# Output projection of a two-layer trunk: the last two token tiles add x in one DVE step, and half of their affine steps for h go to ACT

## The chip, the cores and the metric

The kernel runs on one core of a Trainium2 chip. TensorE (PE, with its weight loads as PEld), VectorE (DVE), ScalarE (ACT) and GpSimd (POOL) each work off a queue of their own in order; all DMAs of this kernel are issued from SyncE's queue (SP), in order as well. The metric is the device time of one execution in microseconds (us), as the median of several. The profile comes from one execution.

## The reference, cut to what matters

Two layers work on 128 context tokens (`x_prompt`) and 1024 latent tokens (`x_sample`), 1024 channels each. What follows is one layer, cut to the parts around the change:

```python
mod = (silu(cvec) @ w_mod + b_mod).reshape(-1, 1, 3 * D_MODEL)
shift, scale, gate = jnp.split(mod, 3, axis=-1)
h = rms_norm(x, g_pre) * (1.0 + scale) + shift
fx, fz, rq, rk, rv, rz, aq, ak, av, az, mg = split_columns(h @ w_in)
...
merged = ga * (ya @ w_pa) + gb * (yb @ w_pb) + gc * (yc @ w_pc)
out = merged @ w_out
x = x + gate * rms_norm(out, g_post)
```

`rms_norm(v, g)` is `v * (mean(v*v) + 1e-6) ** -0.5 * g`, the mean over the 1024 channels. So after the output projection of layer 0 each token gets a new x, and from it the h of layer 1, on which every projection of layer 1 rests.

## The kernel before

**Tiles.** The 1152 tokens are nine tiles of 128 (t = 0 is the context, t = 1 to 8 the latents). h is held in SBUF for all tokens, transposed (channels on partitions), as a pair of rounded high and low parts, HH and HL. A projection is three matmuls for each of eight channel groups (high by high, low by high, high by low): `proj_n` (L223) gives 128 tokens by 512 columns, 24 matmuls, `proj_t` (L214) gives 128 columns by 384 tokens. Weights come as units of 128x1024: a DMA into one of two `raw` tiles, a cast on ACT (L174), a subtraction on POOL (L175).

**The output projection** (L1195 to L1247) runs over the nine tiles. For one tile: `proj_n` twice, columns 0 to 511 into a bank `pj` (of two; for tiles 0 to 3 other banks serve too) and 512 to 1023 into a bank `sl` (of two). ACT squares each half and sums it (L1219). DVE adds the two sums (L1222) and scales them, POOL raises the mean to the power -1/2 (`rstd_of`, L244 to L249), which gives r. DVE then makes acc * r * gate for each half (L1239: reads PSUM and the gate row `gpb`), POOL adds x to that over 1024 columns (L1242), and SP stores x: to `x_d` (scr_x) in layer 0 (L1246), to the output in layer 1 (L1244). One case is written otherwise: the last tile of the last layer (`end`, L1223). There DVE multiplies each half by the gate as soon as its projection is there (`xg`, L1226 and L1229), and when r has come one DVE step for each half makes xg * r + x (L1232), with a store for each half.

**h for layer 1.** In layer 0 `make_h` (L259 to L278) follows for each tile: ACT squares and sums x (L254), DVE and POOL make the power, DVE scales x by it (L256), PE transposes eight 128x128 blocks (L268) into two banks `tr`, DVE makes the affine step with scale `smn` and shift `shn` for each block (L272, four for each half), ACT casts the half to HH (L277), DVE subtracts to get HL (L278).

**What comes next.** Layer 1 begins with `nat_group` (L510): again `proj_n` for t = 0 to 8, into the same two `pj` banks. ACT empties the bank of t = 0 (L525); for t > 0 DVE empties it with the rotary step (`rope`, L482 and L488), which reads the table `ropet`, and ACT takes the rest (L539). After that come units for the Fourier branch by `proj_t` (L641, evacuated by L643 and L644). Between them run steps of the modulation for the next layer, `mod_steps` (L422): loads `mw` (L411), products on DVE (L435, L437), a reduction (L453), stores to `scr_mod` (L463), and small constants of the retention branch (L561 to L612).

**Order and memory.** The order on each engine is worked out when the program is built: a planner with its own model of time puts an instruction into its engine's queue when that model has it ready, the one traced first being preferred. On the chip each queue then runs in that order and waits at its head. SBUF pools are stacked from the left and from the right end, and a tile in a pool that is opened later waits for the release of every earlier tile whose bytes it covers. In the program's memory map (bytes of a partition) the left side in layer 0's output projection is `wo1` (129152 to 137344), `wo2` (to 170112) and `wo3` (170112 to 197184; last in it are the small tiles of `make_h` and `hf`, whose order is that of their first use). On the right side layer 1 opens `wx` (212960 to 229344) and `mix` (197600 to 212960). The table `ropet` is the first tile of `mix`: 197600 to 201696. It is loaded once for layer 1, by L508 (512 KB). A tile `xg` takes 4096 bytes; before, only layer 1's `wo3` holds one.

Of the kernel before, what the change touches and what calls it, by code (L numbers as in the profile page):

```python
# [11 lines left out]
AF = mybir.ActivationFunctionType  # L12
# [4 lines left out]
P = 128  # L17
D = 1024
KT = 8
NT = 9  # L20
# [62 lines left out]
def hybrid_step(ctx, tc, ins, cst, outs):  # L83
    nc = tc.nc
    PE, ACT, DVE, POOL, SP = nc.tensor, nc.scalar, nc.vector, nc.gpsimd, nc.sync
# [7 lines left out]
    def pool(name, bufs=1, side=None, space=None):  # L93
        kw = dict(name=nm(name), bufs=bufs, reuse_waits="tile")
        if side is not None:
            kw["side"] = side
        if space is not None:
            kw["space"] = space
        return tc.tile_pool(**kw)

    def dram(name, shape):
        return nc.dram_tensor(name, shape, F32, kind="Internal").ap()

    def mk(pl, shape, tag, dt=F32, **kw):
        return pl.tile(shape, dt, tag=tag, name=nm(tag), **kw)
# [6 lines left out]
    x_d = dram("scr_x", (TOK, D))  # L112
# [26 lines left out]
    def tr(shape):  # L139
        return bank("tr", 2, shape)  # L140
# [8 lines left out]
    sh = mk(const, [P, KT, 2], "sh")  # L149
    sm = mk(const, [P, KT, 2], "sm")  # L150
    siluc = mk(const, [P, KT, 2], "siluc")
    shn = mk(const, [P, KT, 2], "shn")
    smn = mk(const, [P, KT, 2], "smn")
# [5 lines left out]
    def f(ap):  # L159
        return ap.bitcast(F32)  # L160
# [62 lines left out]
    def proj_n(units, t, acc):  # L223
        tok = slice(t * P, (t + 1) * P)
        for k in range(KT):
            hi, lo = units[k // 2]
            a, b = HH[:, k, tok], HL[:, k, tok]
            PE.matmul(acc, a, hi[:, k % 2, :], start=(k == 0), stop=False)  # L228
            PE.matmul(acc, a, lo[:, k % 2, :], start=False, stop=False)  # L229
            i = PE.matmul(acc, b, hi[:, k % 2, :], start=False, stop=(k == KT - 1))  # L230
        anchor["pe"] = i.ins
# [12 lines left out]
    def rstd_of(pl, ss, n, inv_n, eps, tag):  # L244
        v = mk(pl, [P, n], tag + "v", bufs=2)
        DVE.tensor_scalar(v, ss, inv_n, eps, op0=ALU.mult, op1=ALU.add)
        r = mk(pl, [P, n], tag + "r", bufs=2)
        POOL.tensor_tensor(out=r, in0=v, in1=mhalf[:, :n], op=ALU.pow)
        return r  # L249

    def norm_x(pl, xt):
        xh = mk(pl, [P, D], "xh", bufs=2)
        ss = mk(pl, [P, 1], "ss", bufs=2)
        ACT.activation(xh, xt, AF.Square, accum_out=ss)  # L254
        r = rstd_of(pl, ss, 1, 1.0 / D, EPS, "hr")
        DVE.tensor_scalar(xh, xt, r, None, op0=ALU.mult)  # L256
        return xh

    def make_h(pl, xt, t, sm, sh):  # L259

        s = 0 if t == 0 else 1
        xh = norm_x(pl, xt)
        tok = slice(t * P, (t + 1) * P)
        for half in range(2):
            pt = tr([P, 4, P])
            for kk in range(4):
                k = half * 4 + kk
                PE.transpose(pt[:, kk, :], xh[:, k * P : (k + 1) * P], ident)  # L268
            hf = mk(pl, [P, 4, P], "hf")
            for kk in range(4):  # L270
                k = half * 4 + kk
                DVE.tensor_scalar(  # L272
                    hf[:, kk, :], pt[:, kk, :], sm[:, k, s : s + 1], sh[:, k, s : s + 1],
                    op0=ALU.mult, op1=ALU.add,
                )
            ks = slice(half * 4, half * 4 + 4)
            ACT.copy(HH[:, ks, tok], hf)  # L277
            DVE.tensor_tensor(out=HL[:, ks, tok], in0=hf, in1=f(HH[:, ks, tok]), op=ALU.subtract)  # L278
# [216 lines left out]
    for l in range(DEPTH):  # L495
        last = l == DEPTH - 1
# [704 lines left out]
        wo3 = est.enter_context(pool("wo3"))  # L1201
# [3 lines left out]
        for t in range(NT):  # L1205
            s = 0 if t == 0 else 1
            xo = mk(wo3, [P, D], "xo", bufs=2)
            if l == 0:
                SP.dma_start(xo, ins["x_prompt"][0] if t == 0 else ins["x_sample"][0, (t - 1) * P : t * P, :])
            else:  # L1210
                SP.dma_start(xo, x_d[t * P : (t + 1) * P, :])
            tokP = slice(t * P, (t + 1) * P)
            accs = []
            ss = mk(wo3, [P, 2], "oss2", bufs=2)
            xn = mk(wo3, [P, D], "xh", bufs=2)
            for n, W in enumerate((W0, W1)):
                acc = (sl if n else (pj, pj, sc, pv)[t] if t < 4 else pj)([P, 512])
                proj_n(W, t, acc)
                ACT.activation(xn[:, n * 512 : n * 512 + 512], acc, AF.Square, accum_out=ss[:, n : n + 1])  # L1219
                accs.append(acc)  # L1220
            s1 = mk(wo3, [P, 1], "s1", bufs=2)
            DVE.tensor_tensor(out=s1, in0=ss[:, 0:1], in1=ss[:, 1:2], op=ALU.add)  # L1222
            end = last and t == NT - 1  # L1223
            if end:
                xg = mk(wo3, [P, D], "xg")
                DVE.tensor_tensor(out=xg[:, 0:512], in0=accs[0], in1=gpb[:, s, 0:512], op=ALU.mult)  # L1226
            r = rstd_of(wo3, s1, 1, 1.0 / D, 4.0 * EPS, "xr")
            if end:
                DVE.tensor_tensor(out=xg[:, 512:D], in0=accs[1], in1=gpb[:, s, 512:D], op=ALU.mult)  # L1229
                for n in range(2):  # L1230
                    ns = slice(n * 512, n * 512 + 512)
                    DVE.scalar_tensor_tensor(  # L1232
                        out=xo[:, ns], in0=xg[:, ns], scalar=r, in1=xo[:, ns], op0=ALU.mult, op1=ALU.add
                    )
                    SP.dma_start(y_s[0, (t - 1) * P : t * P, ns], xo[:, ns])
                continue
            for n in range(2):
                ns = slice(n * 512, n * 512 + 512)
                DVE.scalar_tensor_tensor(  # L1239
                    out=xn[:, ns], in0=accs[n], scalar=r, in1=gpb[:, s, ns], op0=ALU.mult, op1=ALU.mult  # L1240
                )
            POOL.tensor_tensor(out=xo, in0=xo, in1=xn, op=ALU.add)  # L1242
            if last:
                SP.dma_start(y_p[0] if t == 0 else y_s[0, (t - 1) * P : t * P, :], xo)  # L1244
            else:
                SP.dma_start(x_d[t * P : (t + 1) * P, :], xo)  # L1246
                make_h(wo3, xo, t, smn, shn)  # L1247
# [31 lines left out]
```

## Time and profile before

| | us |
|---|---|
| median of 3 runs | 2003.23 |
| lowest and highest of them | 2001.77 and 2006.81 |
| the profiled execution, whole | 2004.05 |
| its span, first to last instruction | 2002.3 |
| of the span: PE busy | 1961.0 |
| DVE busy | 991.0 |
| ACT busy | 678.1 |
| POOL busy | 549.0 |

Between the span and the profiled execution's time lie 1.75 us that the profile doesn't show. The busy times are sums over all stages. The stage that the diff touches in layer 0 lies at about 929 to 1063 us of the span (output projection and the h of layer 1, with layer 1's first projection beginning at 1030); that in layer 1 is the last of the span. In a view in order of time a row has start, duration, engine, line, operation, out and in; a bracket at its end gives how long the engine stood idle before it and what ended that. The views of waits give who waited for whom, the sum in us, how often, and the longest.

### The profile page before, as it was taken

The numbers are of one execution on the slowest core, as the hardware profiler recorded it, in microseconds if no ns is written. First come the engines' busy times: TensorE is split into PE (matmuls) and PEld (weight loads), VectorE is DVE, ScalarE is ACT, GpSimd is POOL, SyncE is SP. The second block draws the span as 40 slices with busy tenths as digits, with TensorE's granted clock in tenths as the row PEclk, the third lists the DMA queues.
The fourth block names the chain that finished last, engine by engine and source line by source line (L and its number), as shares of the span: only waits on it lengthen the run. The fifth ranks groups of instructions, "written<-read, shape, count | busy, mean of one in ns | idle before, by whom it ended". The sixth has DMA issues, their size and how long they took to land.

```text
span 2002.3 us, 29865 instructions
## 1 busy us (share of the span) xinstructions
PE 1961.0 (98%) x11046; PEld 1794.2 (90%) x11046; DVE 991.0 (49%) x2557; ACT 678.1 (34%) x1536; POOL 549.0 (27%) x424
## 2 busy tenths in 40 slices
PE   8999999999999999999999999999999999999998
PEld 2898878999999999999878878899999999999987
DVE  4626556556667765104675272444556665410411
ACT  3522111234555444114331212022455555421411
POOL 2222232111112332444441214122111222333342
PEclk9999999999999999999999999999999999999999
DMA  9323554353334334323344145234422433422142
GB/s 298 105 72 98 149 139 135 102 178 105 97 116 123 117 103 137 91 89 128 116 135 101 58 103 162 74 115 129 125 82 88 121 100 97 143 92 83 60 153 85
DMA packets 245186, 230.53 MB, mean 115 GB/s; under 512 B 37920, under 2 KB 215856, under 8 KB 244784
## 3 DMA queue, kind: packets, MB, share of 16 engines
q1 hardware_dynamic: 245040, 228.62, 37.6%
q8 instruction: 87, 1.43, 0.3%
q14 instruction: 59, 0.48, 0.1%
HBM read 170.14 MB, written 58.42 MB: 114 GB/s over the span
## 4 chain that ended last, share of the span: by engine, by line
PE 88%; DMA 4%; DVE 3%; ACT 1%; issue 1%; SPq 1%; POOL 1%; DVEq 0%; POOLq 0%; ACTq 0%
PE pj L218 13%; PE pj L220 13%; PE pj L219 13%; PE pj L228 5%; PE pj L229 5%; PE pj L230 5%; PE tr L1102 3%; DMA raw<-in_w_in 2%; PE sl L1048 2%; PE pv L1109 2%; PE pv L1108 2%; PE sl L951 2%; PE sl L953 2%; PE sl L952 2%; PE pj L951 2%; PE pj L952 2%
## 5 line engine op out<-in xcount | busy, mean ns | idle before, releaser
L218 PE MATMUL pj<-HH,uh 128*128 128x384 f32 x1440 | 491.0, 341 | 9.0 <-DVE XL L644 4.2
L219 PE MATMUL pj<-HL,uh 128*128 128x384 f32 x1440 | 485.4, 337 | 0.0
L220 PE MATMUL pj<-HH,ul 128*128 128x384 f32 x1440 | 485.3, 337 | 0.0
L175 POOL TENSOR_TENSOR ul<-raw,uh 128x1024 fp32r<-128x1024 f32 x80 | 192.4, 2406 | 491.1 <-ACT uh L174 400.0
L218 PEld LDWEIGHTS pj<-HH,uh 128*128 128x128 f32 x1440 | 271.0, 188 | 14.2 <-ACT mth L948 4.9
L219 PEld LDWEIGHTS pj<-HL,uh 128*128 128x128 f32 x1440 | 271.2, 188 | 1.6
L220 PEld LDWEIGHTS pj<-HH,ul 128*128 128x128 f32 x1440 | 270.9, 188 | 1.5
L174 ACT CAST uh<-raw 128x1024 fp32r<-128x1024 f32 x80 | 84.0, 1049 | 172.3 <-PE pj L219 123.6
L437 DVE SCALAR_TENSOR_TENSOR macc<-mw,siluc,macc 128x256 f32<-128x256 f32 x224 | 134.7, 644 | 8.2 <-DMA mw<-in_w_mod 8.2
L228 PE MATMUL pj<-uh,HH 128*128 128x512 f32 x336 | 133.7, 399 | 3.7 <-ACT kv L537 1.8
L229 PE MATMUL pj<-ul,HH 128*128 128x512 f32 x336 | 132.8, 395 | 0.0
L230 PE MATMUL pj<-uh,HL 128*128 128x512 f32 x336 | 132.3, 394 | 0.0
L954 DVE SCALAR_TENSOR_TENSOR M<-M,sl 128x384 f32<-128x384 f32 x48 | 26.6, 554 | 202.2 <-PE sl L953 197.1
L1085 ACT ACTIVATE E<-E,NM 128x640 f32<-128x640 f32 (+1 forms) x128 | 101.9, 798 | 66.5 <-DVE NM L1081 66.4
L1106 DVE TENSOR_TENSOR El<-tr,Eh 128x512 fp32r<-128x512 f32 x132 | 89.0, 685 | 45.9 <-ACT Eh L1105 45.6
L1105 ACT CAST Eh<-tr 128x512 fp32r<-128x512 f32 x132 | 74.7, 587 | 86.8 <-PE tr L1102 85.1
L966 POOL TENSOR_TENSOR mth<-mth,ml 128x384 f32<-128x384 f32 x48 | 51.7, 1077 | 178.0 <-DVE mth L954 122.5
L1102 PE MATMUL tr<-ident,E 128*128 128x128 f32 x528 | 84.0, 272 | 0.2 <-ACT E L1085 0.2
L954 DVE SCALAR_TENSOR_TENSOR mth<-mth,pj 128x384 f32<-128x384 f32 x96 | 52.9, 551 | 63.1 <-ACT mth L948 31.9
L966 POOL TENSOR_TENSOR M<-M,mrow 128x384 f32<-128x384 f32 x48 | 48.7, 1015 | 123.1 <-DVE M L954 73.5
L1066 DVE CUSTOM_DVE_ANT_0 E<-sl,mask,m 128x384 f32<-128x384 f32 (+1 forms) x128 | 72.1, 579 | 17.4 <-PE sl L1048 17.0
L228 PEld LDWEIGHTS pj<-uh,HH 128*128 128x128 f32 x336 | 63.3, 188 | 19.2 <-ACT kv L537 1.9
(312 smaller groups left out, 4038.4 us busy)
## 6 DMA issues: line engine op xcount, KB each, us to landing
raw<-in_w_in SPq DMA_DIRECT2D x84, 512.0 KB
scr_m<-mth SPq DMA_DIRECT2D x96, 192.0 KB
mw<-in_w_mod SPq DMA_DIRECT2D x128, 128.0 KB
scr_n<-ns SPq DMA_DIRECT2D x36, 256.0 KB
ml<-scr_m SPq DMA_DIRECT2D x48, 192.0 KB
mrow<-scr_m SPq DMA_DIRECT2D x16, 576.0 KB
big<-in_w_mod SPq DMA_DIRECT2D x16, 512.0 KB
raw<-in_w_out SPq DMA_DIRECT2D x16, 512.0 KB
```

The source lines that it names most:

```text
L175: POOL.tensor_tensor(out=lo, in0=raw, in1=f(hi), op=ALU.subtract)
L218: PE.matmul(acc, hi[:, k, :], HH[:, k, tok], start=(k == 0), stop=False)
L219: PE.matmul(acc, hi[:, k, :], HL[:, k, tok], start=False, stop=False)
L220: i = PE.matmul(acc, lo[:, k, :], HH[:, k, tok], start=False, stop=(k == KT - 1))
L228: PE.matmul(acc, a, hi[:, k % 2, :], start=(k == 0), stop=False)
L229: PE.matmul(acc, a, lo[:, k % 2, :], start=False, stop=False)
L230: i = PE.matmul(acc, b, hi[:, k % 2, :], start=False, stop=(k == KT - 1))
L437: DVE.scalar_tensor_tensor(out=accs[s], in0=w, scalar=siluc[:, k, s : s + 1], in1=accs[s], op0=ALU.mult, op1=ALU.add,)
L966: POOL.tensor_tensor(out=th, in0=th, in1=ml, op=ALU.add)
L1085: ACT.activation(Es[hh][:, 0:nk], srcs[hh], AF.Exp, bias=NM[t][:, hs + hh : hs + hh + 1], scale=0.125, accum_out=DEN[t][:, hs + hh : hs + ...
L1102: PE.transpose(pt[:, hh, hp_, :], Es[2 * hp_ + hh][:, n * P : (n + 1) * P], ident)
L1106: DVE.tensor_tensor(out=El, in0=pt, in1=f(Eh), op=ALU.subtract)
```

## The change

In `make_h` a flag lets every second of the affine steps run on ACT (an activation Identity with scale and shift) in place of DVE. In the output projection the case `end` now holds for the last two tiles (t = 7 and 8) of both layers. In layer 0 the two tiles so make `xg`, then x by one DVE step for each half, store x whole and call `make_h` with the flag. In layer 1 tile 7 does as tile 8 did before. The addition on POOL (L1242) is left out for these tiles.

```diff
--- before.py
+++ after.py
@@ -256,7 +256,7 @@
         DVE.tensor_scalar(xh, xt, r, None, op0=ALU.mult)
         return xh
 
-    def make_h(pl, xt, t, sm, sh):
+    def make_h(pl, xt, t, sm, sh, both=False):
 
         s = 0 if t == 0 else 1
         xh = norm_x(pl, xt)
@@ -269,6 +269,11 @@
             hf = mk(pl, [P, 4, P], "hf")
             for kk in range(4):
                 k = half * 4 + kk
+                if both and kk % 2:
+                    ACT.activation(
+                        hf[:, kk, :], pt[:, kk, :], AF.Identity, bias=sh[:, k, s : s + 1], scale=sm[:, k, s : s + 1]
+                    )
+                    continue
                 DVE.tensor_scalar(
                     hf[:, kk, :], pt[:, kk, :], sm[:, k, s : s + 1], sh[:, k, s : s + 1],
                     op0=ALU.mult, op1=ALU.add,
@@ -1220,7 +1225,7 @@
                 accs.append(acc)
             s1 = mk(wo3, [P, 1], "s1", bufs=2)
             DVE.tensor_tensor(out=s1, in0=ss[:, 0:1], in1=ss[:, 1:2], op=ALU.add)
-            end = last and t == NT - 1
+            end = t >= NT - 2
             if end:
                 xg = mk(wo3, [P, D], "xg")
                 DVE.tensor_tensor(out=xg[:, 0:512], in0=accs[0], in1=gpb[:, s, 0:512], op=ALU.mult)
@@ -1232,7 +1237,11 @@
                     DVE.scalar_tensor_tensor(
                         out=xo[:, ns], in0=xg[:, ns], scalar=r, in1=xo[:, ns], op0=ALU.mult, op1=ALU.add
                     )
-                    SP.dma_start(y_s[0, (t - 1) * P : t * P, ns], xo[:, ns])
+                    if last:
+                        SP.dma_start(y_s[0, (t - 1) * P : t * P, ns], xo[:, ns])
+                if not last:
+                    SP.dma_start(x_d[t * P : (t + 1) * P, :], xo)
+                    make_h(wo3, xo, t, smn, shn, True)
                 continue
             for n in range(2):
                 ns = slice(n * 512, n * 512 + 512)
```

## Rows read from the trace of the kernel before

**Rows 1.** The page's first part: busy time of each engine over the span, its share and its instructions.

```profile
PE 1961.0 (98%) x11046; PEld 1794.2 (90%) x11046; DVE 991.0 (49%) x2557; ACT 678.1 (34%) x1536; POOL 549.0 (27%) x424
```

**Rows 2.** Three of the waits of PE between 1005 and 1110 us: who waited for what, us in total, times, longest.

```profile
PE tr L268 <- DVE xh L256: 1.7, 1, 1.7
PE pj L228 <- DVE xh L1239: 1.2, 1, 1.2
PE pj L228 <- ACT ns L525: 0.2, 1, 0.2
```

**Rows 3.** PE in order of time: three instructions that waited, the first matmul of layer 1's projection for tile 3 (at 1052.56), and the last matmul of the span.

```profile
1038.10 0.50 PE L228 MATMUL pj<-uh,HH 128*128 128x512 f32 x1 [1.20 <-DVE xh L1239]
...
1049.55 1.09 PE L268 MATMUL tr<-ident,xh 128*128 128x128 f32 x8 [1.66 <-DVE xh L256]
...
1052.56 0.39 PE L228 MATMUL pj<-uh,HH 128*128 128x512 f32 x1
...
1105.94 0.69 PE L218 MATMUL pj<-HH,uh 128*128 128x384 f32 x1 [4.16 <-DVE XL L644]
...
1995.02 0.39 PE L230 MATMUL sl<-w1h,HL 128*128 128x512 f32 x1
```

**Rows 4.** DVE in order of time, 1020 to 1051 us.

```profile
1021.19 0.74 DVE L1239 SCALAR_TENSOR_TENSOR xh<-sl,xrr,gpb 128x512 f32<-128x512 f32 x1
...
1029.30 3.04 DVE L437 SCALAR_TENSOR_TENSOR macc<-mw,siluc,macc 128x256 f32<-128x256 f32 x2
...
1037.96 0.74 DVE L1239 SCALAR_TENSOR_TENSOR xh<-sl,xrr,gpb 128x512 f32<-128x512 f32 x1
...
1038.84 2.40 DVE L577 TENSOR_TENSOR ls<-lu,ld 128x8 f32<-128x8 f32 x1
...
1041.56 1.36 DVE L272 TENSOR_SCALAR hf<-tr,smn,shn 128x128 f32<-128x128 f32 x4
...
1046.64 2.85 DVE L256 TENSOR_SCALAR xh<-xo,hrr 128x1024 f32<-128x1024 f32 x1 [0.18 <-POOL hrr L248]
...
1050.29 0.42 DVE L482 TENSOR_TENSOR ns<-pj,rope 128x256 f32<-128x256 f32 x1
1050.62 0.48 DVE L488 TENSOR_TENSOR rpb<-pj,rope 128x128 f32<-128x128 f32 x2
```

**Rows 5.** POOL in order of time, 1020 to 1049 us.

```profile
1021.20 2.40 POOL L175 TENSOR_TENSOR ul<-raw,uh 128x1024 fp32r<-128x1024 f32 x1 [0.72 <-ACT uh L174]
1023.56 2.40 POOL L1242 TENSOR_TENSOR xo<-xo,xh 128x1024 f32<-128x1024 f32 x1
...
1029.66 2.40 POOL L175 TENSOR_TENSOR ul<-raw,uh 128x1024 fp32r<-128x1024 f32 x1
...
1038.83 2.39 POOL L1242 TENSOR_TENSOR xo<-xo,xh 128x1024 f32<-128x1024 f32 x1 [2.69 <-DVE ld L575]
1046.06 0.55 POOL L248 TENSOR_TENSOR hrr<-hrv,mhalf 128x1 f32<-128x1 f32 x1 [4.84 <-DVE lq L583]
1046.57 2.37 POOL L175 TENSOR_TENSOR xl<-raw,xh 128x1024 fp32r<-128x1024 f32 x1
```

**Rows 6.** ACT in order of time, 1027 to 1044 us.

```profile
1027.05 0.58 ACT L1219 ACTIVATE xh<-pj 128x512 f32<-128x512 f32 x1
...
1042.95 0.62 ACT L277 CAST HH<-hf 128x512 fp32r<-128x512 f32 x1 [5.77 <-DVE hf L272]
1043.48 0.58 ACT L525 COPY ns<-pj 128x512 f32<-128x512 f32 x1
```

**Rows 7.** Groups of ACT instructions by line and shape over the span: times, busy us, mean ns of one, idle before.

```profile
L1085 ACT ACTIVATE E<-sl,NM 128x128 f32<-128x128 f32 x16 | 5.8, 367 | 4.1 <-DVE NM L1081 4.1
...
L537 ACT COPY kv<-pj 128x128 f32<-128x128 f32 x16 | 4.3, 267 | 53.2 <-DVE rpb L488 27.0 <-DMA scr_n<-kv 18.3 <-DMA scr_n<-ns 7.8
```

**Rows 8.** The end of layer 1, the last tile's step on DVE in order of time: `xg`, then x.

```profile
1990.81 0.69 DVE L1226 TENSOR_TENSOR xg<-pj,gpb 128x512 f32<-128x512 f32 x1 [3.04 <-ACT xh L1219]
...
1997.72 1.41 DVE L1232 SCALAR_TENSOR_TENSOR xo<-xg,xrr,xo 128x512 f32<-128x512 f32 x2 [0.73 <-POOL xrr L248]
```

**Rows 9.** The load of the table `rope` in layer 1 (L508): times, ns to issue, when.

```profile
L508 SPq DMA_DIRECT2D rope<-cst_rope x1: 368/368/368, 926.5 to 926.5; - x1
```

**Rows 10.** The longest piece of the chain that ended last that was a load of weights, 512 KB: start, us.

```profile
1092.20 11.66 DMA raw<-in_w_in
```

**Rows 11.** Busy time by stretch: PE, PEld, DVE, ACT, POOL (with how many instructions), granted clock, busy share of the DMA engines, GB/s.

```profile
1036.00:1039.00 3.00, 1.80 (x8) 1.15 (x8) 2.00 (x7) 0.21 (x1) 0.31 (x2) 1.00 0.72 200
1039.00:1042.00 3.00, 3.00 (x15) 2.42 (x14) 2.93 (x5) 0.00 (x0) 2.22 (x1) 1.00 1.14 323
1042.00:1045.00 3.00, 2.81 (x13) 1.99 (x12) 2.86 (x11) 2.05 (x4) 0.00 (x0) 1.00 0.79 261
...
1106.00:1108.00 2.00, 2.00 (x6) 2.00 (x7) 1.83 (x3) 0.00 (x0) 1.42 (x1) 0.50 0.01 4
1108.00:1110.00 2.00, 2.00 (x10) 2.00 (x10) 0.00 (x0) 0.00 (x0) 0.00 (x0) 0.73 0.61 194
...
1112.00:1116.00 4.00, 4.00 (x24) 3.91 (x23) 1.35 (x3) 0.35 (x1) 0.00 (x0) 1.00 0.11 35
...
90.00:1036.00 946.00, 934.71 (x5350) 870.05 (x5349) 516.01 (x1295) 323.31 (x731) 268.79 (x204) 0.99 0.38 116
...
1112.00:2002.00 890.00, 877.63 (x5064) 820.70 (x5062) 378.18 (x999) 295.41 (x685) 240.65 (x188) 1.00 0.34 104
```

## The prediction

> **What bounds the kernel now.** I read the page first: PE is busy for 1961.0 of 2002.3 us [rows 1], so the kernel is as long as its matmuls, and a change to DVE, POOL and ACT can only move the 41 us in which PE stands. Next come PE's own waits where layer 0 passes into layer 1: 1.7, 1.2 and 0.2 us [rows 2] and a longer one of 4.16 us behind them. The view of PE in order of time gives their places [rows 3], and the other engines in order of time say why. The first three hang on the two tiles that the diff touches:
>
> - 1.20 us before 1038.10 [rows 3]: layer 1's projection of tile 1 needs the `pj` bank of tile 8, which the old step holds until r is there and DVE has run L1239 at 1037.3. ACT had squared what stood in it at 1027.05 [rows 6].
> - 0.2 us [rows 2]: the next bank, emptied on ACT at 1043.48, stands behind the cast of tile 7's half h, and that had waited 5.77 us for DVE [rows 6]. DVE had stood in L577 for 2.40 us, on 128x8 elements, while POOL added x of tile 8 [rows 4, 5].
> - 1.66 us before 1049.55 [rows 3]: tile 8's transposes wait for L256, which took 2.85 us beside POOL's L175 [rows 4, 5].
>
> The fourth, 4.16 us before 1105.94 [rows 3], belongs to the Fourier units: ACT waits for a weight load that took 11.66 us [rows 10]. Behind it PE runs at a granted clock of 0.50, its lower level of 1.2 GHz, and then 0.73 as it climbs back to 2.4: 16 matmuls in 4 us where it later makes 24 [rows 11], so 8 x 4/24 = 1.3 us more. No such loss follows the short waits (clock 1.00 in the stretches from 1036 to 1045).
>
> **The change, part by part.**
>
> *x on DVE (layer 0, tiles 7 and 8).* Removed: two additions on POOL, 2.40 us each [rows 5]. Added: two `xg` steps a tile at 0.69 = 1.38 us of DVE [rows 8]. The two L1232 (1.41 us for both [rows 8]) replace two L1239 (0.74 for one [rows 4]), even. The `xg` of the first half needs no r: it follows ACT's square of that half, which ran at 1027.05 [rows 6], so the bank is free near 1028 to 1030, long before PE wants it at 1036.9. (`xg` has one buffer; tile 7's last read of it comes about 1022 to 1024, before tile 8 writes.) **The 1.20 us go.** x is there when L1232 ends, where L1239 ended before: 1037.96 + 0.74 = 1038.7 for tile 8, against 1038.83 + 2.39 = 1041.2 on POOL [rows 4, 5]. With that addition gone nothing holds L577, so tile 7's affine steps come 2.2 us earlier and **the 0.2 us go.**
>
> *Half of the affine steps on ACT.* DVE drops 4 of 8 a tile: 2 x 1.36 / 2 = 1.36 us [rows 4], which pays for `xg`. ACT gets four a tile. The trace has no such Identity from PSUM with scale and shift from memory; a plain copy of that shape takes 267 ns, an Exp with one such operand 367 [rows 7], so 100 ns an operand and about 0.47 us for two: 0.93 us a half beside 0.68 on DVE. Bounds: 0.27 and 0.8 each. The half is done 0.4 us sooner (between 0.8 sooner and 0.3 later), and the cast behind it stays on ACT. PE doesn't wait for this h: its tiles 7 and 8 are the last that layer 1 projects. What queues behind the new ACT steps is the evacuation L525; it comes earlier because DVE does.
>
> *Tile 8's transposes.* L256 ended at 1049.49, 8.3 us after x. From 1038.7 the same distance gives 1047.0, and less the 2.2 us of L577, 1044.8. PE arrives at 1049.55 - 1.66 - 1.4 = 1046.5 if they keep their place in its order. But the planner puts them where its model has x ready, so up to the POOL addition's 2.4 us sooner: 1044.1. What is left of the 1.66 us is 0 to 0.7; if POOL's L175 again starts right behind the power, as at 1046.57, up to 2.9. I take 0.7, the row without a new block being the nearer. For tile 7, whose transposes didn't wait before [rows 2], the same move allows 0 to 2.4; I take 0.6.
>
> *A block of its own.* L1239 ran its 0.74 us beside POOL's L175 from 1021.20 unhindered, one input being PSUM [rows 4, 5]. Steps with all inputs in SBUF did not: two L437 took 3.04 us beside the L175 of 1029.66, L577 2.40, L256 2.85. L1232 is of the second sort, and its only row (1.41 us) has no POOL work beside it [rows 8]. Price: 0 to 2.4 us for a tile, for tile 7 above all, where an L175 stands ready at 1021.20. That is tile 7's 0 to 2.4 again, not to be counted twice. The Trainium skill, SBUF — State Buffer, Who interferes with whom, says this as a rule: a DVE instruction with two SBUF inputs contends with a GpSimd instruction that reads SBUF, one with at most one doesn't, and the later one fully blocks. The rows agree. By that rule alone both tiles would pay, and the sum would end near no change.
>
> *The table `rope`.* The diff says nothing of it, but `xg` now takes 4096 bytes in layer 0 too, behind `hf`: 197184 to 201280, and the table of layer 1 begins at 197600. Its load went out at 926.5 [rows 9]; now it must wait until tile 8's L1232 has read `xg`, about 1038.7 (if the planner puts other DVE work in between, 1041.2, when x was done before). On SP's queue, what is behind it waits too: weights of the Fourier units, which PE doesn't use before nine tiles are projected, and `mw`. Who needs the table is tile 1's L482, and its bank is wanted by tile 3 at 1052.56 [rows 3], after the gain at 1049.5. From 1039 to 1045 the DMA engines already move 3 us x 323 GB/s and 3 us x 261 GB/s, that is 1.75 MB at a mean of 292 GB/s [rows 11]. With 0.52 MB more and the table last it lands 7.8 us after 1039, at 1046.8; L482 and L488 take 0.9 [rows 4], so the bank is free at 1047.7: no wait, 1.8 us to spare. Upper end: issue at 1041.2 and 11.66 us, the slowest load of the chain [rows 10], lands at 1052.9 and frees the bank at 1053.8: 4.3 us of wait and, as that is as long as the wait at 1106, 1.3 us of clock. I take 0, the row of the same stretch being nearer than one 55 us on.
>
> *Layer 1, tile 7.* POOL loses an addition that nothing waits for, DVE gets 1.38 us more in a stretch where it has waited 3.04 us for its next step [rows 8], and there is one store more. Tile 8's `xg` at 1990.81 [rows 8] comes a whole tile later than tile 7's last read of it. PE's end and the tail behind it stay. Worth 0.
>
> *Sum.* -1.20 - 0.2 - 1.66 + 0.7 + 0.6 = -1.76, about -1.8 us: what comes 1.8 us earlier at 1052 stays so, since the loads behind the wait at 1106 hang on PE's last matmuls of that projection. The profiled execution took 2004.05 us (span 2002.3 and 1.75 around it), so 2002.3 for it. It lies 0.8 above the median of the three runs, 2003.23; on that median the forecast is **2001.4 us**. About 0.3% (6 us) is what a measurement here can tell from no change.
>
> **The rivals.**
>
> 1. *The table comes late (slower).* Mechanism as above. For it: the bytes overlap, and DVE's queue around 1036 is full. Against: 1.8 us to spare. It decides once the table lands after 1048.6, and costs at its upper end 4.3 + 1.3 = 5.6 us against 3.06 gained: +2.6, 2005.8 us.
> 2. *The blocks take it all.* L1232 and L256 lose 2.4 us to L175 on one tile or two, or PE meets the moved transposes before xh; or ACT's half merely waits, so that the second half of the diff does nothing. For it: L175 filled POOL's gap each time [rows 5]. Against: POOL has 4.8 us less to do. The waits change their names, 2003.2 us.
> 3. *The wait at 1106 goes too.* If the new order issues that weight load sooner, or ACT's evacuation stands before its cast, another 4.2 + 1.3 us go: -1.8 - 5.5 = -7.3, 1995.9 us. For it: a wait behind an in-order queue turns on the order alone. Against: nothing in the diff touches it.
> 4. *Layer 1 is laid out worse.* The planner lays out all that follows anew. The same code left PE idle for 11.3 us in layer 0 (90 to 1036) and for 12.4 - 6.6 = 5.8 us in layer 1 (1112 to 2002, less what follows PE's last matmul, which ends at 1995.4) [rows 3, 11]: an order can cost 5.5 us. -1.8 + 5.5 = +3.7, 2006.9 us.
>
> **How the numbers follow.** Forecast (a gain of 0.5 to 3.1 us, 2000.1 to 2002.7) 0.43, rival 1 0.13, rival 2 0.24, rival 3 0.12, rival 4 0.08. The range reaches most of the way to rival 3 and over rival 4: 1996.5 to 2007. Faster by over 0.3% (under 1997.2) is rival 3 alone: 0.12. Slower (over 2009.2) needs rivals 1 and 4 together, or an order worse by more than the one comparison shows: 0.07, most of it rival 4's. The rest, 0.81, lies within 0.3%.
>
> **What would show it.** Right, if in the changed kernel's waits of PE the one for L1239 at tile 1's bank is gone, x of tile 8 comes near 1039, L577 takes under 0.2 us, and the table's load goes out after tile 8's L1232 with no wait of PE behind L482. Wrong, if PE waits for the table, if L1232 takes 2 us or more beside L175, if the transposes of tiles 7 and 8 wait for over 1.5 us together, or if PE's idle time after 1112 differs from 12.4 us by more than 2.

## The result and the profile after

The changed kernel took **2016.75 us**, the median of 4 runs (2013.71 to 2017.91); the kernel before took 2002.5 us beside it (median of 4, 2000.49 to 2006.81). The ratio is 1.0072, 95% interval 1.0052 to 1.0091: slower by 14 us. The forecast was 2001.4 us, the range ended at 2007.0, and "slower" had 0.07. The prediction was wrong.

The profiled execution took 2017.91 us (span 2016.1). Below L271 the lines of its code stand 5 to 9 further down than before: L530 is the old L525 (ACT empties the bank of layer 1's tile 0), L487 and L493 the rope steps, L513 rope's load, L273 and L277 the affine steps on ACT and DVE, L282 the cast to HH, L1237 the x step.

The page's busy times of the changed kernel, which answer to [rows 1]:

```profile
PE 1963.5 (97%) x11046; PEld 1797.2 (89%) x11046; DVE 990.4 (49%) x2555; ACT 680.8 (34%) x1544; POOL 543.7 (27%) x421
```

PE is busy 2.5 us longer, but the span grew by 13.8: most of the loss is time in which PE stands. Its waits where the layers meet, 1000 to 1125 us (us in total, times, longest), which answer to [rows 2]:

```profile
PE pj L228 <- ACT ns L530: 10.7, 1, 10.7
PE pj L218 <- DVE XL L649: 2.9, 1, 2.9
PE tr L268 <- ACT hf L273: 2.4, 1, 2.4
PE tr L268 <- DVE lq L588: 1.8, 1, 1.8
```

The wait for tile 8's bank (1.20 us) is gone, as forecast. In the place of the 0.2 us for ACT's evacuation stand 10.7. PE in order of time there, to be laid beside [rows 3]:

```profile
1039.48 0.63 PE L268 MATMUL tr<-ident,xh 128*128 128x128 f32 x4 [1.79 <-DVE lq L588]
1044.20 0.66 PE L268 MATMUL tr<-ident,xh 128*128 128x128 f32 x4 [2.37 <-ACT hf L273]
1055.56 0.80 PE L228 MATMUL pj<-uh,HH 128*128 128x512 f32 x1 [10.70 <-ACT ns L530]
1056.16 0.63 PE L229 MATMUL pj<-ul,HH 128*128 128x512 f32 x1
...
1059.90 0.40 PE L229 MATMUL pj<-xl,HH 128*128 128x512 f32 x1
1060.13 0.39 PE L230 MATMUL pj<-xh,HL 128*128 128x512 f32 x1
```

After the long wait matmuls start 0.43 us apart, later 0.23 (the granted clock there stands in the last row of the windows below). Why did the bank come so late? ACT in order of time, up to the evacuation, and what DVE and SP did for the rope steps (three views: ACT, DVE, SP's queue):

```profile
1052.98 0.46 ACT L273 ACTIVATE hf<-tr,shn,smn 128x128 f32<-128x128 f32 x1 [1.34 <-DVE hf L277]
1053.92 0.46 ACT L273 ACTIVATE hf<-tr,shn,smn 128x128 f32<-128x128 f32 x1 [0.48 <-DVE hf L277]
1054.41 0.62 ACT L282 CAST HH<-hf 128x512 fp32r<-128x512 f32 x1
1054.93 0.58 ACT L530 COPY ns<-pj 128x512 f32<-128x512 f32 x1
```

```profile
1052.47 0.41 DVE L277 TENSOR_SCALAR hf<-tr,smn,shn 128x128 f32<-128x128 f32 x1
1053.47 0.41 DVE L277 TENSOR_SCALAR hf<-tr,smn,shn 128x128 f32<-128x128 f32 x1 [0.59 <-ACT hf L273]
1055.06 0.69 DVE L283 TENSOR_TENSOR HL<-hf,HH 128x512 fp32r<-128x512 f32 x1 [1.18 <-ACT HH L282]
1055.67 0.42 DVE L487 TENSOR_TENSOR ns<-pj,rope 128x256 f32<-128x256 f32 x1
```

```profile
1045.30 0.37 SPq L188 DMA_DIRECT2D raw<-in_w_in  x1
1045.72 0.57 SPq L513 DMA_DIRECT2D rope<-cst_rope  x1
```

L530 has no bracket: it waited for nothing of its own. It copies a bank that PE filled long before, and needs no rope. It stands in ACT's queue behind the last cast of tile 8's h; in the kernel before it stood behind the first cast of tile 7 [rows 6]. L487 stands just so on DVE, behind the last step of h. Rope's load went out at 1045.7, against 926.5 before [rows 9].

And when was the table there? Windows of the changed kernel (PE, PEld, DVE, ACT, POOL busy, granted clock, DMA share, GB/s):

```profile
1045.00:1047.00 2.00, 0.00 (x0) 0.00 (x0) 1.93 (x11) 1.43 (x6) 0.28 (x1) 0.78 0.11 31
1047.00:1049.00 2.00, 0.00 (x0) 0.00 (x0) 2.00 (x8) 0.58 (x2) 0.00 (x0) 0.50 1.07 318
1049.00:1051.00 2.00, 0.00 (x0) 0.00 (x0) 2.00 (x4) 1.60 (x4) 0.00 (x0) 0.50 0.70 174
1051.00:1053.00 2.00, 0.00 (x0) 0.00 (x0) 1.20 (x3) 0.64 (x2) 0.00 (x0) 0.50 0.00 0
...
1055.50:1059.50 4.00, 3.94 (x9) 3.15 (x10) 2.98 (x9) 0.38 (x2) 0.00 (x0) 0.50 0.47 163
```

2 us x (31 + 318 + 174) GB/s = 1.05 MB, the weight and the table (0.52 MB each); from 1051 to 1053 nothing moves. So the table had landed by 1051, and its first reader ran at 1055.67. The queues' order held it, not the load.

**A stretch to compare by.** Whole times of one kernel scatter by up to 14 us from run to run (e2: 1994.8 to 2008.5). In the 13 profiled executions of this study layer 0's output projection ended anywhere from 1022.7 to 1030.1, and from the last Fourier matmul (L653 before, L658 after) to PE's last matmul it took 830.7 to 837.1. Before and after have the same order on PE outside the place where the layers meet. So I compare the stretch between the last matmul of layer 0's projection (`sl<-w1h`) and the last of layer 1's first Fourier matmuls (`sl<-MFh` or `MFl`), start to start. The last matmul of layer 0's projection in PE's order of time, before and then after:

```profile
1030.09 0.39 PE L230 MATMUL sl<-w1h,HL 128*128 128x512 f32 x1
```

```profile
1025.11 0.39 PE L230 MATMUL sl<-w1h,HL 128*128 128x512 f32 x1
```

Before: 1164.32 - 1030.09 = 134.2 us. After: 1172.03 - 1025.11 = 146.9. The 12.7 us between them are nearly the whole loss of 14, and the waits give it: 17.8 us after less 7.3 before (1.7 + 1.2 + 0.2 + 4.2) is 10.5; the ten steps from the matmul start at 1055.56 to that at 1059.90 took 4.34 us where ten at 0.23 take 2.3, that is 2.0 more. Together 12.5. (Behind the wait of the Fourier units both ran for some 3.4 us at a clock of 0.50, so that cancels.) The stretch has a scatter of its own: e9 and e11, below, have the order of the kernel before on PE throughout and took 131.5. In them the Fourier wait was 2.9 us for 4.2, and the clock behind it stayed at 1.00. So differences of up to 3 us in the last column of the table say nothing by themselves.

### The profile page after: what moved, and what is told of

The parts are those of the page before. It is cut to its first block, busy times and chain, and to the rows that moved or that the text cites. A ratio compares the mean times of both kernels' runs of the same rounds, so it can differ in the third digit from the quotient of the medians.

```text
span 2016.1 us, 29877 instructions
## 1 busy us (share of the span) xinstructions
PE 1963.5 (97%) x11046; PEld 1797.2 (89%) x11046; DVE 990.4 (49%) x2555; ACT 680.8 (34%) x1544; POOL 543.7 (27%) x421
## 4 chain that ended last, share of the span: by engine, by line
PE 87%; DMA 4%; DVE 4%; ACT 1%; issue 1%; SPq 1%; POOL 1%; DVEq 0%; POOLq 0%; ACTq 0%
PE pj L218 13%; PE pj L220 13%; PE pj L219 13%; PE pj L228 5%; PE pj L229 5%; PE pj L230 5%; PE tr L1107 3%; PE sl L1053 2%; DMA raw<-in_w_in 2%; PE pv L1114 2%; PE pv L1113 2%; PE sl L956 2%; PE sl L958 2%; PE sl L957 2%; PE sl L230 2%; PE sl L229 2%
## 5 line engine op out<-in xcount | busy, mean ns | idle before, releaser
L175 POOL TENSOR_TENSOR ul<-raw,uh 128x1024 fp32r<-128x1024 f32 x80 | 192.6, 2409 | 504.1 <-ACT uh L174 463.6
L174 ACT CAST uh<-raw 128x1024 fp32r<-128x1024 f32 x80 | 84.0, 1050 | 173.6 <-PE pj L219 125.5
L442 DVE SCALAR_TENSOR_TENSOR macc<-mw,siluc,macc 128x256 f32<-128x256 f32 x224 | 135.1, 646 | 9.5 <-DMA mw<-in_w_mod 9.5
L971 POOL TENSOR_TENSOR M<-M,mrow 128x384 f32<-128x384 f32 x48 | 48.9, 1020 | 122.5 <-DVE M L959 67.0
```

The source lines that it names most:

```text
L175: POOL.tensor_tensor(out=lo, in0=raw, in1=f(hi), op=ALU.subtract)
L442: DVE.scalar_tensor_tensor(out=accs[s], in0=w, scalar=siluc[:, k, s : s + 1], in1=accs[s], op0=ALU.mult, op1=ALU.add,)
L971: POOL.tensor_tensor(out=th, in0=th, in1=ml, op=ALU.add)
```

## The experiments

**Theory 1.** `xg` takes 4096 bytes behind `hf` and so covers the first bytes of the pool `mix`, in which rope lies. What waits is not rope alone but the whole pool, `ns` with it: the planner takes `mix` as free only once layer 0's last pool is done, which in its order is when tile 8's h is done. So it lays the evacuation (it writes `ns`) and the rope steps behind all h work. **Theory 2.** The affine steps shared by ACT and DVE take turns and make h, and all behind it, late. **Theory 3.** The new x steps are blocked by POOL.

| kernel | covers rope? | median us | ratio to before, 95% | rope's load issued | stretch us |
|---|---|---|---|---|---|
| before | no | 2002.5 | | 926.5 | 134.2 |
| after | yes | 2016.75 | 1.0072 (1.0052 to 1.0091) | 1045.7 | 146.9 |
| e1 unread tile alone | yes | 2015.98 | 1.0064 (1.0048 to 1.0080) | 1044.4 | 145.1 |
| e2 change, xg without bytes of its own | no | 2001.10 | 0.9989 (0.9975 to 1.0002) | 919.1 | 128.9 |
| e3 x step alone | yes | 2016.74 | 1.0069 (1.0052 to 1.0087) | 1045.2 | 148.4 |
| e4 change, rope in its own pool | yes | 2012.80 | 1.0048 (1.0031 to 1.0065) | 1047.7 | 143.9 |
| e5 ACT half alone | no | 2005.71 | 1.0018 (1.0005 to 1.0031) | 919.6 | 135.1 |
| e6 x step alone, xg as in e2 | no | 2002.07 | 1.0003 (0.9990 to 1.0016) | 919.1 | 132.7 |
| e7 as e2, each bank read by one engine | no | 2001.90 | 0.9994 (0.9982 to 1.0007) | 919.2 | 133.1 |
| e8 unread tile, used at 951 only | yes | 2011.94 | 1.0047 (1.0028 to 1.0066) | 1044.9 | 144.5 |
| e9 unread tile, 384 bytes | no | 2002.39 | 1.0005 (0.9994 to 1.0015) | 920.7 | 131.5 |
| e10 unread tile, 448 bytes | yes | 2016.03 | 1.0068 (1.0055 to 1.0081) | 1046.9 | 145.3 |
| e11 layer 1's part alone | no | 2003.18 | 1.0001 (0.9991 to 1.0012) | 920.8 | 131.5 |

Kernels that were measured together share the runs of the kernel before (medians 2003.61 for e1 to e4, 2001.16 for e5 to e8, 2002.55 for e9 to e11).

**e1, the overlap without the change** (before):

```diff
             POOL.tensor_tensor(out=xo, in0=xo, in1=xn, op=ALU.add)
+            if not last and t >= NT - 2:
+                pad = mk(wo3, [P, D], "xg")
+                DVE.tensor_copy(pad[:, D - 8 : D], xn[:, 0:8])
```

> The kernel before, to which layer 0's output projection gets a tile of 4096 bytes for token tiles 7 and 8, in the place that xg has in the changed kernel (197184 to 201280, over the first bytes of the next layer's rope); DVE copies 8 columns into it that nobody reads. Neither x nor the affine steps are changed. Theory 1 (the overlap alone: the planner holds the whole pool of the next layer's projection, rope and ns with it, until layer 0's pool is done, so ACT's evacuation of tile 1's bank queues behind all h work): 2010 to 2018 us, PE waits 8 to 12 us for that evacuation near 1050. Theory 2 (the affine steps of one PSUM bank on two engines take turns and make h late): as before, 2000 to 2005. Theory 3 (the new steps of x are blocked by POOL): as before, 2000 to 2005.

An unread tile costs 0.64%, nearly the whole loss. (The texts on record call L525 the evacuation of tile 1's bank. It empties tile 0's, which the projection of tile 2 waits for.) One number was missed: the wait for the evacuation was 5.4 us and not 8 to 12, but in front of it stands one of 6.0 for the transposes of tile 8 (e10, below, has nearly the same rows). The stretch is as long.

**e2, the change without the overlap** (after):

```diff
-                xg = mk(wo3, [P, D], "xg")
+                xg = mk(wo3, [P, D], "xg") if last else xn
```

> The changed kernel with xg of layer 0 in the tile that the squares are written to, so that it takes no bytes of its own and overlaps nothing of the next layer; all else of the change stays. Theory 1: 1997 to 2004 us, rope's load out near 925 as before and the 10.7 us wait gone. Theory 2: 2010 or more, since the affine steps are still shared. Theory 3: 2008 or more, since x is made by the same steps.

Theory 1's number, and theories 2 and 3 fall as the cause: every step of the change is still there, and 15 us are gone. ACT and DVE in order of time show the order that the planner finds when `mix` is free:

```profile
1035.37 0.62 ACT L282 CAST HH<-hf 128x512 fp32r<-128x512 f32 x1
1035.89 0.58 ACT L530 COPY ns<-pj 128x512 f32<-128x512 f32 x1
1039.18 0.45 ACT L273 ACTIVATE hf<-tr,shn,smn 128x128 f32<-128x128 f32 x1
```

```profile
1045.02 0.41 DVE L487 TENSOR_TENSOR ns<-pj,rope 128x256 f32<-128x256 f32 x1
1045.36 0.47 DVE L493 TENSOR_TENSOR rpb<-pj,rope 128x128 f32<-128x128 f32 x2
1045.75 0.40 DVE L277 TENSOR_SCALAR hf<-tr,smn,shn 128x128 f32<-128x128 f32 x1
```

The evacuation is back behind tile 7's first cast, and the rope step of tile 1 comes between steps of tile 8's h. PE's waits from 1000 to 1125 us:

```profile
PE tr L268 <- DVE lq L588: 1.5, 1, 1.5
PE tr L268 <- ACT hf L273: 1.4, 1, 1.4
PE pj L228 <- ACT ns L544: 0.5, 1, 0.5
```

That is 3.4 us where the layers meet, against 3.1 in the kernel before [rows 2]: the change without the overlap gains nothing there. The wait for the Fourier units, 4.2 us before, is not among them.

**e3, the x step alone** (after):

```diff
-                    make_h(wo3, xo, t, smn, shn, True)
+                    make_h(wo3, xo, t, smn, shn)
```

> The changed kernel without its second half: all affine steps stay on DVE, x of tiles 7 and 8 is made on DVE with xg in bytes of its own. Theory 1: 2010 to 2018 us, with a PE wait of 7 to 12 us for the evacuation of tile 1's bank, as xg overlaps rope as before. Theory 2: 1999 to 2005. Theory 3: 2010 to 2018, but with the waits at the transposes of tiles 7 and 8 and not at the evacuation.

Slower by as much, with 7.1 us of wait for the evacuation and 3.9 for tile 8's xh: the ACT half of the diff is not needed for the loss.

**e4, rope in a pool of its own** (after):

```diff
-        ropet = mk(mp, [P, 8, P], "rope")
+        rp = mix.enter_context(pool("rp", side="right"))
+        ropet = mk(rp, [P, 8, P], "rope")
```

> The changed kernel with rope in a pool of its own at the same address; ns, rpb and kv, which overlap nothing, stay in the old one. xg overlaps rope as in the changed kernel. Theory 1: the evacuation of tile 1's bank comes before the h work again; rope is still late, so PE may wait for the rope steps of tile 1's bank as rival 1 of the prediction has it, 0 to 5.6 us: 1999 to 2007 us. If the late table itself is the cause and not what is held with it: 2010 to 2018, with the wait now behind the rope steps. Theory 2 and 3: 2010 or more.

Half of theory 1 held, half missed. The evacuation came early again (L531 at 1040.88, behind tile 7's first cast). But the time stayed 0.48% up, where I expected 2007 us at most: PE waits 7.57 us for tile 1's bank, one later. That is the number, and the place, that I had given to the rival, the late table itself as the cause. Was it the load that came late, or the queue that held its reader? DVE and PE in order of time:

```profile
1057.37 0.68 DVE L283 TENSOR_TENSOR HL<-hf,HH 128x512 fp32r<-128x512 f32 x1
...
1058.57 0.41 DVE L487 TENSOR_TENSOR ns<-pj,rope 128x256 f32<-128x256 f32 x1
```

```profile
1050.38 1.89 PE L634 MATMUL sl<-w,cdft 128*128 128x256 f32 x8
1059.83 0.80 PE L228 MATMUL pj<-uh,HH 128*128 128x512 f32 x1 [7.57 <-ACT ns L545]
```

Windows of the same kernel (columns as above):

```profile
1051.00:1052.00 1.00, 1.00 (x6) 0.76 (x4) 0.64 (x2) 0.68 (x2) 0.00 (x0) 1.00 1.14 336
1052.00:1053.00 1.00, 0.27 (x2) 0.00 (x0) 0.38 (x2) 0.56 (x2) 0.00 (x0) 1.00 0.26 66
1053.00:1054.00 1.00, 0.00 (x0) 0.00 (x0) 0.45 (x1) 0.52 (x1) 0.00 (x0) 1.00 0.00 0
```

The DMA engines are done by 1053, and PE begins to wait at 1052.27. Had the rope steps (0.9 us) and ACT's copy of the rest of the bank (0.4) run at 1053, the wait would have been some 2 us, an estimate from these rows; it was 7.57, because L487 stands on DVE behind L283, the last step of tile 8's h. So it is again the queue, and not the load. Two queues are held, ACT's (`ns`) and DVE's (rope). The rope steps alone cost 0.48% here. In the changed kernel PE's wait ended with the evacuation L530; no run holds `ns` alone.

**e5, the ACT half alone** (before with the diff's `make_h`; layer 0's x step stays as it was):

```diff
-                make_h(wo3, xo, t, smn, shn)
+                make_h(wo3, xo, t, smn, shn, t >= NT - 2)
```

> The kernel before with the second half of the change alone: of tiles 7 and 8 two of four affine steps of each half run on ACT; x is made as before, with POOL's addition, and no xg in layer 0. Theory 1: 2000 to 2006 us (nothing overlaps). Theory 2: 2008 or more, with waits of PE on hf.

Within theory 1's numbers. A little slower (0.18%, at most 0.31% by its interval), and its one longer wait (3.96 us for ACT's L648, before 1093.82) lies in the Fourier units. Why it is slower stays open.

**e6, the x step without overlap or ACT half.** Both edits, of e2 and of e3.

> x of layer 0's tiles 7 and 8 on DVE with xg in the squares' tile (no overlap), all affine steps on DVE. Theory 1: 1998 to 2004 us, as the prediction's sum without the share of ACT: the wait for tile 1's bank (1.2 us) gone. Theory 3: 2006 or more, since x's steps are blocked by POOL as in the changed kernel (4.93 us for the two of tile 7).

No change: the wait for tile 8's bank is gone, and one of 1.36 us for the evacuation stands in its place, with one of 2.33 us for the next bank (L544) behind it. Theory 3 falls, although the block is real: the two x steps of tile 7 took 4.93 us here as in the changed kernel.

**e7, one engine for each bank** (after, with e2's edit):

```diff
-                if both and kk % 2:
+                if both and half:
```

> The changed kernel without the overlap (xg in the squares' tile), and ACT's four affine steps of a tile are all those of its second bank, so that no bank is read by both engines. If sharing a bank costs (theory 2 as a small term): 1 to 3 us less than the same kernel with a shared bank (1996 to 2002). If it costs nothing on PE's path: the same within 1.5 us.

The same within 1.5 us. ACT's four steps in a row, in order of time:

```profile
1036.43 1.48 ACT L273 ACTIVATE hf<-tr,shn,smn 128x128 f32<-128x128 f32 x4
1037.80 0.59 ACT L530 COPY ns<-pj 128x512 f32<-128x512 f32 x1
```

Four take 1.48 us on one engine. Shared, the half at 1052.47 of the changed kernel took until 1054.38, 1.91 us. PE's two waits for the transposes (1.5 and 1.4 us in e2) are gone; others came in their place (2.4 us for a Fourier weight's load, 2.3 for XL).

**e8, the tile used early** (before):

```diff
                 make_h(wo3, xo, t, smn, shn)
+                if t == 0:
+                    pad = mk(wo3, [P, D], "xg")
+                    DVE.tensor_copy(pad[:, D - 8 : D], xn[:, 0:8])
```

> The kernel before, with a tile of 4096 bytes in layer 0's output projection at the place that xg has in the changed kernel, written once for token tile 0 (8 columns, near 945 us) and never used again. If what is held back waits for the last use of the overlapping tile: 2000 to 2005 us, rope's load out near 945. If it waits for the whole pool of layer 0's projection to be done (theory 1): as the kernel with the tile at 7 and 8, 2010 to 2018 us, with the same PE wait.

The tile's only use is at 950.8 (expected near 945), and rope's load still goes out at 1044.9; the waits of PE are those of e1 and e10 (6.0 and 5.4 us). So what counts is not the last use of the covering tile but the end of layer 0's pool, and it counts in the planner's order, not as a wait on the chip: the load went out 10 us before the last step of tile 8's h ran (1055.05). That corrects what stands ahead of the prediction, that a tile waits for the tiles whose bytes it covers. Whether the planner goes by the pool as a whole, or gives up the covering tile only when its pool ends, no run here parts.

**e9 and e10, 64 bytes apart.** The tile of e1 with `[P, 96]` and with `[P, 112]` elements of 4 bytes; rope begins at 197600.

> The kernel before with the unread tile in layer 0's output projection for token tiles 7 and 8, cut to 384 bytes: it ends at 197568, 32 bytes below the next layer's rope. Theory 1: as before, 1999 to 2005 us, rope's load out near 925, no wait of PE for the evacuation of tile 1's bank over 1 us. If the extra tile or its DVE step costs by itself: 2008 or more.

> The same tile with 448 bytes: it ends at 197632 and overlaps rope by its first 32 bytes. Theory 1: the whole loss with 64 bytes more, 2010 to 2018 us, rope's load out near 1044 and the same waits of PE near 1050 as with 4096 bytes. If the loss grows with the bytes that overlap or with the time for which they are in use: 2000 to 2006.

PE's waits from 1000 to 1125 in e9 and then in e10, each with the row of rope's load:

```profile
PE pj L218 <- DVE XL L644: 2.9, 1, 2.9
PE tr L268 <- DVE xh L256: 1.7, 1, 1.7
PE pj L228 <- DVE xh L1239: 1.2, 1, 1.2
PE pj L228 <- ACT ns L525: 0.2, 1, 0.2
L508 SPq DMA_DIRECT2D rope<-cst_rope x1: 368/368/368, 920.7 to 920.7; - x1
```

```profile
PE tr L268 <- DVE xh L256: 6.0, 1, 6.0
PE pj L228 <- ACT ns L525: 5.4, 1, 5.4
PE pj L218 <- DVE XL L644: 2.9, 1, 2.9
PE pj L228 <- DVE xh L1239: 1.3, 1, 1.3
L508 SPq DMA_DIRECT2D rope<-cst_rope x1: 534/534/534, 1046.9 to 1046.9; - x1
```

With 32 bytes to spare, the three waits of [rows 2], to the tenth. With 32 bytes too many, the whole loss. Neither the size of the overlap nor how long the tile is used makes the loss (e8 cost 0.47% by its ratio and e10 0.68%, with intervals that overlap); that there is an overlap does.

**e11, layer 1's part** (before):

```diff
-            end = last and t == NT - 1
+            end = last and t >= NT - 2
```

> The kernel before with the new x step in layer 1's tile 7 alone; layer 0 is untouched. The prediction's step (worth 0): 1999 to 2005 us, no new wait of PE over 1 us after 1990. If layer 1 is laid out worse, or the store and POOL's lock cost there (rival 4): 2006 to 2009.

Worth nothing, as forecast.

## Why the prediction was wrong

**The step that failed** is the term for the table `rope`, taken as 0 with 5.6 us as its upper end. The overlap was seen. The load was reckoned too early: counted from the last matmul of layer 0's projection (1030.09 before, 1025.11 after), it was to go out 8.6 to 11.1 us later and to land 16.7 to 22.8 us later. It went out 20.6 us later, on SP's queue behind the weight load of 1045.30, which I hadn't counted, and landed 23.9 to 25.9 us later (between 1049 and 1051). But the price lay elsewhere: what failed is the reckoning that L482 runs as soon as the table has landed, and that only L482 hangs on it. The planner holds the whole pool (e8 and e10; in e4, with rope in another pool, the evacuation was free again), so both the rope steps and the evacuation L525, which reads no table, were queued behind all h work of tiles 7 and 8. I wrote that the evacuation "comes earlier because DVE does"; it came last. The 0.2 us that were to go became 10.7, and the clock 2.0 more. Rival 1 named the right overlap, but it priced a wait for L482 at tile 3 (e4 shows that one, 7.6 us), and the wait that came was for the evacuation at tile 2. It took its price, 5.6 us, from a row of a load, where the length of the queue counts; the stretch lost 12.7. (Its +2.6 is 2.5 by its own terms, 5.6 - 3.06.)

**Step by step.**
- The 1.20 us for tile 8's bank are gone. Right.
- L577 (now L582) took 0.15 us for 2.40. Right.
- x of tile 8 was ready 11.3 us after layer 0's last projection matmul (1035.02 + 1.41 - 1025.11); before, 1041.22 - 1030.09 = 11.1. Not sooner, so wrong: DVE's sum for r came 7.0 us after that matmul where it had come 5.0 after it, laid behind seven steps of the modulation, of which the first had waited 1.32 us for its load and four took 3.81 us beside POOL's L175. That took back the 2.4 us of POOL's addition.
- Tile 8's transposes: 1.66 us were to become 0.7, and tile 7's were to cost 0.6. Tile 7's cost nothing, tile 8's 1.79 + 2.37 = 4.2 (the row of the first names L588; L256, which makes xh of tile 8, had ended 0.15 us before it). The planner moved them up by more than the 2.4 us that I allowed, and the second of the two banks was freed late by the shared affine steps of tile 7: ACT's first one there stood in ACT's queue behind a cast (L174, 1041.81) that had waited 3.15 us for a weight load. So a step moved to ACT took on ACT's waits too.
- One ACT step was put at 0.47 us and took 0.46. But the half was to be done 0.4 us sooner (0.3 later at worst), and it took 1.91 us against 1.36 on DVE alone [rows 4], 0.55 later: the engines take turns. The brackets of L273 and L277 above show each waiting for the other, and [rows 8] had shown it: DVE's `xg` step, idle for 3.04 us before it, was released by ACT's square of the same bank, and the two share nothing else. The Trainium skill, PSUM — Partial Sum Buffer, section PSUM bank collisions raise a hardware error, says that a compiler's scheduler makes any two engines take turns on the same partitions of one bank, reads against reads too; the rows agree. For L273 and L277 no run here parts the bank from the tile `hf` that both engines write.
- The block of rival 2 came on tile 7: L1237 took 4.93 us beside two L175 in a row, 3.5 more (priced at up to 2.4) than the 1.41 of tile 8, which had no POOL work beside it. PE didn't wait for it. The prediction says that a DVE step with at most one SBUF input doesn't contend with POOL. That is too wide for these rows: L256 reads one SBUF tensor and a scalar for each partition, and still took 2.85 us beside L175 [rows 4], against 0.75 at 1038.58 of the changed kernel with POOL idle.

```profile
1017.04 4.93 DVE L1237 SCALAR_TENSOR_TENSOR xo<-xg,xrr,xo 128x512 f32<-128x512 f32 x2
...
1035.02 1.41 DVE L1237 SCALAR_TENSOR_TENSOR xo<-xg,xrr,xo 128x512 f32<-128x512 f32 x2
```

```profile
1016.21 5.21 POOL L175 TENSOR_TENSOR ul<-raw,uh 128x1024 fp32r<-128x1024 f32 x2 [0.24 <-ACT uh L174]
```

- Layer 1: 0, shown by e11. Rival 4 didn't come: from the end of that first projection on, PE's order is the same in both kernels.
- The wait near 1106 went from 4.2 to 2.9 us, with the code's order around it unchanged, and in e9 and e11 it is 2.9 too. Rival 3 was seen in e2: no wait there. (In e5 one of 4.0 us for L648 stands in its place.)

**Without the overlap** the sum's number came near, and that is luck. e2 is 2.2 us faster by its ratio (2002 x 0.0011), with an interval from 5.0 us faster to 0.4 slower, and -1.8 was the sum. But where the layers meet, e2's waits are 3.4 us against 3.1 before, and the sum had left 1.3 of them (0.7 + 0.6): the 1.20 us went, and the transposes took 2.9. What shortens e2's stretch is the Fourier wait that isn't there, which the sum didn't count (rival 3): against e9 its stretch is 2.6 us shorter, 2.9 less there and 0.3 more here. Whether the change took that wait away or chance did, one profile doesn't show. And 2.2 us is no measurable gain: no version here beats the kernel before beyond its interval.

## What to carry to other kernels

When an edit adds a tile, compare the end of its pool with the start of the pool that opens next on those bytes: with this planner 32 covered bytes laid the work on two tiles of that pool behind all work on the old one. Price such an overlap by the in-order queues, as the work that the held instructions are laid behind, and not by the transfer that is late. And a scratch tile that is dead at that point (here the squares' dump) gives the same step without a byte.

## What the runs showed of the hardware that was not expected

- The granted clock fell while PE stood for 10.7 us: it was 0.78 in 1045 to 1047, then 0.50, the lower level of 1.2 GHz, and the ten steps after the wait cost 2.0 us more. Through the waits of 1.8 and 2.4 us before it the clock stayed at 1.00 (1036 to 1045). The length of a wait alone doesn't tell: in e6 the clock was 0.50 from 1046 to 1049, behind a wait of 2.3 us, in e7 0.53 from 1039 to 1042.5, behind one of 2.4, while in e9 it was 1.00 from 1098 to 1106, behind one of 2.9.
- A step shared by two engines that read one PSUM bank ran longer (1.91 us) than on one engine alone (1.36 on DVE, 1.48 on ACT).
- The same instructions in the same order differ by several us from one execution to another: the last matmul of layer 0's output projection started at 1030.1 before and at 1024.4 in e11, which differ in layer 1 alone.
